# Split weights of k and q stored during the first MLP, and attention outputs summed by an accumulating DMA

## The chip, the cores and the metric

The kernel runs on one core of one Trainium2 chip. The metric is the device time of one execution in microseconds. Engines: PE is the matrix engine (TensorE), DVE the vector engine, ACT the scalar engine, POOL is GpSimd, and SP is the queue that issues most DMAs. Each engine works off its own instructions in order; semaphores tie them together.

## The reference

A decoder of two layers over 1024 tokens of width 1024, float32. Layer 0 mixes by an S5 state-space block, layer 1 by a stick-breaking attention of 16 heads of 64; each mixer is followed by an MLP with squared ReLU of width 4096, and both by a layer norm on a weighted residual.

```python
x = layer_norm(ALPHA * x + mix, ...)           # after s5_mixer or attention
ff = squared_relu_mlp(x, w1, b1, w2, b2)       # square(relu(x @ w1 + b1)) @ w2 + b2
x = layer_norm(ALPHA * x + ff, ...)
...
k, v = split(x @ w_kv)                         # once, after layer 0
q = (x @ w_q)
z = einsum("qd,kd->qk", qb, kb) * scale        # blocks of 128 queries, per head
log_1mb = where(causal, log_sigmoid(-z), 0)
suffix = cumsum(log_1mb, reverse=True) - log_1mb
w = where(causal, exp(log_sigmoid(z) + suffix), 0)
out = einsum("qk,kd->qd", w, vb)               # heads side by side, then out @ w_out
```

## The kernel before

PE multiplies rounded float32 (fp32r). To keep precision every operand is split into a high part, its cast to fp32r, and a low part, the remainder: `split` (L121) casts on ACT (L122) and subtracts on DVE (L123). Each product is three multiplies: high x high, high x low, low x high. A split weight is one tile of 128 x 2 x 512, both parts side by side, 512 KB; the raw weight is 256 KB.

The stages follow each other: the S5 layer (to about 505 us), the up-projection of the first MLP, `mlp_up` (505 to 807), its down-projection, `Down` (807 to 1117), the projection of v, `VProject` (to 1213), the first projections of k and q (to 1242), the attention loop (to 1668), the out-projection `proj_ln` (to 1762) and the second MLP (to 2419).

**First MLP.** `mlp_up` runs 104 steps; each multiplies x by one operand made from the weights (a plan of seven products for four blocks). Operands are split ahead into slots, eight tiles named "w", four in pool `wa` and four in `wb`, handed out in turn by `sl.next()`. `down.ahead` (L1034) is called at each step and does, beside it, what the down-projection needs: it loads the residual `xm_d` in 16 halves, scales them, adds a bias and stores them back (tiles `d0ya` in the pool `pf`, tag "p", four buffers), and at the end loads the first weights of the down-projection into the same buffers.

**k and q.** `project_all` is a generator of units; `load_p` (L1379) loads a weight of k or q for a pair of heads p raw, in two halves `r_k` or `r_q`, and splits it into two slots of `wa`, one projection ahead of its use. The first, `wk0`, is loaded in `VProject.run` behind the fifth of the last eight multiplies by `w_v`. There are 8 pairs, so 16 weights and 32 splits. 33 units run ahead of the loop, the others inside it.

**Attention loop.** 128 `Step`s, 16 heads x 8 query tiles, a software pipeline. `scores` multiplies q by k (`pz`, L1436 and L1437), ACT makes two sigmoids of it, `qq` (L1438) and `be`, and POOL masks their diagonal blocks (`affine_select`, L1441). `weights`, one step later, runs DVE's product scan over `qq` (L1447) and multiplies `be` by it (L1448). `trans` transposes `be` on PE in pieces (`pt`, L1460) and splits them (`wTh` by ACT, `wTl` by DVE). `out`, once for two query tiles, multiplies by v (`po`, L1474). The high and the low part of v lie side by side as 128 columns, so `po` has two halves of 64 rows: high v times both parts of the weights, and low v times their high part. Their sum is the head's output. ACT copies both to `ob` (L1476), and SP stores them apart to `o_d[0]` and `o_d[1]` in memory (L1478). POOL also issues the loads of v (L1426) and the copies that stack k and q for a head (L1410), into its queue in order.

**Out-projection.** `load_o` (L1499) loads both halves of 128 rows of the output (`ol`), adds them on DVE (L1503) and splits the sum into `oT`. Seven are called during the last part of the loop by `out_ahead`, the others behind it.

What order the instructions have on an engine is set by a scheduler that lays out the program by readiness and by the place in which the code stands.

## Time and profile before

| | us |
|---|---|
| median of 3 runs | 2428.63 |
| lowest, highest | 2428.26, 2428.94 |
| the profiled execution's own time | 2421.34 |
| its span | 2419.6 |
| PE, DVE, ACT, POOL busy in the span | 2274.4, 1842.8, 1211.6, 540.0 |
| mean granted clock of PE | 0.984 |

The profiled execution is one run, 7.3 us under the median of the others; its span is the time from its first instruction to its last. Busy time is time in which an engine had an instruction running; PE is busy for 94% of the span, DVE for 76%, but these are means over stages that are bound in different ways. A row `X <- Y` under waits says that X stood idle and that Y's end let it go.

### The profile page before, as it was taken

To read this page: it belongs to the slowest core of one execution; us is meant where nothing else is said; L and a number is where in the kernel's file an instruction comes from. 1 tells how busy PE (TensorE), PEld (TensorE's weight loads), DVE (VectorE), ACT (ScalarE), POOL (GpSimd) and SP (SyncE) were. 2 spreads that over 40 slices of the span, in tenths; PEclk is the share of its full clock that TensorE was granted. 3 is DMA by queue.
4 is the path that set the end of the run, shared out by engine and by line. 5 is a ranking of instruction groups with operands and counts; after the bars stand their busy time and mean duration, and the time that the engine had idled before them with its cause. 6 is when DMAs were issued, how large, how long until landed. Compare 5 with 4: busy or idle time off the path is not lost.

```text
span 2419.6 us, 32714 instructions
## 1 busy us (share of the span) xinstructions
PE 2274.4 (94%) x11040; PEld 1860.3 (77%) x11040; DVE 1842.8 (76%) x2868; ACT 1211.6 (50%) x2283; POOL 540.0 (22%) x796
## 2 busy tenths in 40 slices
PE   9887799999999999999999999988989999999996
PEld 7666677777888788887888788766767888788885
DVE  8778664797665788789259999897788666687888
ACT  5344452366555444445147667673357555444443
POOL 6556430012112100001134443341002211100001
PEclk9989899999999999999999999999999999999998
DMA  4222131366444755435665555555358444665433
GB/s 148 56 64 58 40 121 62 110 224 232 144 144 165 251 180 166 147 101 147 131 157 118 121 130 125 120 134 187 113 182 290 156 156 146 224 206 165 132 115 106
DMA packets 195161, 349.39 MB, mean 144 GB/s; under 512 B 23216, under 2 KB 66224, under 8 KB 194992
## 3 DMA queue, kind: packets, MB, share of 16 engines
q1 hardware_dynamic: 136112, 246.61, 32.4%
q0 software_dynamic: 58880, 100.69, 15.0%
q8 instruction: 87, 1.43, 0.2%
q14 instruction: 82, 0.67, 0.1%
HBM read 212.96 MB, written 100.66 MB: 130 GB/s over the span
## 4 chain that ended last, share of the span: by engine, by line
PE 64%; DVE 12%; issue 5%; DMA 4%; POOL 2%; ACT 2%; SPq 0%; POOLq 0%; DVEq 0%; ACTq 0%
PE d0M L1096 4%; PE d0M L1097 4%; PE d0M L1098 4%; PE d1M L1096 4%; PE d1M L1098 4%; PE d1M L1097 4%; DVE qq L1447 2%; PE m1A L832 2%; PE m1A L834 2%; PE m1A L833 2%; PE m0A L832 2%; PE m0A L833 2%; PE m0A L834 2%; DVE be L1448 2%; PE po L1474 1%
## 5 line engine op out<-in xcount | busy, mean ns | idle before, releaser
L1447 DVE TENSOR_TENSOR_SCAN qq<-qq 128x128 f32<-128x128 f32 (+7 forms) x128 | 174.2, 1363 | 11.4 <-POOL qq L1441 11.1
L1096 PE MATMUL d1M<-w_d12M,w_d1HM 128*128 128x512 f32 x448 | 174.9, 391 | 3.9 <-DVE d1y L1105 3.9
L1096 PE MATMUL d0M<-w_d02M,w_d0HM 128*128 128x512 f32 x448 | 174.6, 390 | 1.6 <-ACT w_d02M L122 1.2
L1098 PE MATMUL d1M<-w_d12M,w_d1HM 128*128 128x512 f32 x448 | 175.2, 391 | 0.0
L1097 PE MATMUL d1M<-w_d12M,w_d1HM 128*128 128x512 f32 x448 | 174.7, 390 | 0.0
L1097 PE MATMUL d0M<-w_d02M,w_d0HM 128*128 128x512 f32 x448 | 174.5, 389 | 0.0
L1098 PE MATMUL d0M<-w_d02M,w_d0HM 128*128 128x512 f32 x448 | 174.3, 389 | 0.0
L192 POOL TENSOR_TENSOR rsd<-ved,nhalf 128x1 f32<-128x1 f32 x16 | 16.2, 1014 | 621.5 <-DVE ved L190 613.3
L122 ACT CAST w_d1HM<-d1hM 128x512 fp32r<-128x512 f32 x110 | 68.3, 621 | 170.1 <-PE d1M L1098 148.3
L122 ACT CAST w_d0HM<-d0hM 128x512 fp32r<-128x512 f32 x110 | 68.3, 621 | 169.1 <-PE d0M L1098 143.6
L122 ACT CAST wTh<-pt 128x512 fp32r<-128x512 f32 (+1 forms) x192 | 88.0, 485 | 81.4 <-PE pt L1460 80.9
L1460 PE MATMUL pt<-ident,be 128*128 128x128 f32 x576 | 90.5, 281 | 34.8 <-DVE wTl L123 25.8
L1460 PEld LDWEIGHTS pt<-ident,be 128*128 128x128 f32 x576 | 69.7, 143 | 60.9 <-issue 18.5
L123 DVE TENSOR_TENSOR w_d1HM<-d1hM,w_d1HM 128x512 fp32r<-128x512 f32 x110 | 75.9, 690 | 52.4 <-ACT w_d1HM L122 52.2
L123 DVE TENSOR_TENSOR w_d0HM<-d0hM,w_d0HM 128x512 fp32r<-128x512 f32 x110 | 75.9, 690 | 51.6 <-ACT w_d0HM L122 51.5
L123 DVE TENSOR_TENSOR wTl<-pt,wTh 128x512 fp32r<-128x512 f32 (+1 forms) x192 | 99.5, 545 | 9.9 <-ACT wTh L122 9.9
L1448 DVE TENSOR_TENSOR be<-be,qq 128x127 f32<-128x127 f32 (+7 forms) x128 | 99.4, 777 | 7.2 <-POOL be L1441 0.7
L1096 PEld LDWEIGHTS d1M<-w_d12M,w_d1HM 128*128 128x128 f32 x448 | 84.1, 188 | 24.1 <-ACT w_d12M L122 4.3
L1438 ACT ACTIVATE qq<-pz 128x512 f32<-128x512 f32 (+1 forms) x192 | 96.8, 504 | 10.8 <-DVE be L1448 5.6
L1096 PEld LDWEIGHTS d0M<-w_d02M,w_d0HM 128*128 128x128 f32 x448 | 84.1, 188 | 21.4 <-DVE d0y L1105 2.5
L1098 PEld LDWEIGHTS d1M<-w_d12M,w_d1HM 128*128 128x128 f32 x448 | 84.1, 188 | 18.4
L1097 PEld LDWEIGHTS d1M<-w_d12M,w_d1HM 128*128 128x128 f32 x448 | 84.1, 188 | 17.8
(477 smaller groups left out, 7162.4 us busy)
## 6 DMA issues: line engine op xcount, KB each, us to landing
d0hM<-h_d SPq DMA_DIRECT2D x110, 256.0 KB, 2.7
d1hM<-h_d SPq DMA_DIRECT2D x110, 256.0 KB, 2.7
x1ring<-in_w SPq DMA_DIRECT2D x70, 256.0 KB, 3.2
x3ring<-in_w SPq DMA_DIRECT2D x70, 256.0 KB, 3.2
h_d<-m0hs POOLq DMA_DIRECT2D x64, 256.0 KB, 3.1
h_d<-m1hs POOLq DMA_DIRECT2D x64, 256.0 KB, 2.6
d0r<-in_w SPq DMA_DIRECT2D x58, 256.0 KB, 3.5
d1r<-in_w SPq DMA_DIRECT2D x58, 256.0 KB, 3.7
```

The source lines that it names most:

```text
L122: act.copy(hi, src)
L123: dve.tensor_sub(lo, src, hi)
L832: pe.matmul(ps_, wh, xh[:, k], start=first and k == 0, stop=False, skip_group_check=True)
L833: pe.matmul(ps_, wh, xl[:, k], start=False, stop=False, skip_group_check=True)
L834: pe.matmul(ps_, wl, xh[:, k], start=False, stop=k == 3, skip_group_check=True)
L1096: pe.matmul(ps_, hh[:, tok(t)], wh, start=first, stop=False, skip_group_check=True)
L1097: pe.matmul(ps_, hh[:, tok(t)], wl, start=False, stop=False, skip_group_check=True)
L1098: pe.matmul(ps_, hl[:, tok(t)], wh, start=False, stop=last, skip_group_check=True)
L1438: act.activation(qq[:, s0:s1], pz, AF.Sigmoid, scale=-0.125)
L1447: dve.tensor_tensor_scan(out=rev, data0=rev, data1=rev, initial=1.0, op0=ALU.mult, op1=ALU.bypass)
L1448: dve.tensor_mul(be[:, 0:ns - 1], be[:, 0:ns - 1], qq[:, 1:ns])
L1460: pe.transpose(pt[:, b_], self.be[:, tok(s0 + b_)], ident)
```

## The change

Two parts.

The weights of k and q are split during the first MLP. A job `SplitKQ` is called from `down.ahead`; for each of 32 halves it loads the raw half into a buffer of `pf`, splits it two steps later into a slot of `sl`, and SP stores the 512 KB to `kq_d` in memory. The first load is at step 13, and one follows each two or three steps; the last half is split at step 92. `load_kq` then loads the split weights straight into the slots where `load_p` split them.

The halves of a head's output are added in memory. `o_d` has one half; SP stores the first 64 rows of `ob`, and POOL issues a DMA that adds the other 64 rows to the same place, one `out` later. `load_o` loads once and does not add.

```diff
--- before.py
+++ after.py
@@ -78,7 +78,8 @@
-    o_d = drp.tile([2, D, S], F32, name="o_d")
+    o_d = drp.tile([D, S], F32, name="o_d")
+    kq_d = drp.tile([2, KD, 2, P, 2, HF], F32, name="kq_d")
@@ -995,7 +996,7 @@
-            down.ahead(i, NSTEPS, xo.ring)
+            down.ahead(i, NSTEPS, xo.ring, sl)
@@ -1016,7 +1017,8 @@
-        def __init__(self, l, nm, xd, wb, last, then=None):
+        def __init__(self, l, nm, xd, wb, last, then=None, job=None):
+            self.job = job
@@ -1031,8 +1033,10 @@
-        def ahead(self, i, n, ring):
-
+        def ahead(self, i, n, ring, sl):
+            if self.job:
+                self.job.step(i, self.pf, sl)
@@ -1243,6 +1247,33 @@
+    class SplitKQ:
+        PARTS = [(y, p, c) for p in range(KD) for y in range(2) for c in range(2)]
+        def __init__(self):
+            self.raw = {}
+        def step(self, i, pl, sl):
+            for j, (y, p, c) in enumerate(self.PARTS):
+                i0 = 13 + 5 * j // 2
+                if i == i0:
+                    self.raw[j] = pl.tile([P, HF], F32, tag="p", name=f"kq{j}")
+                    dma.dma_start(self.raw[j], A[("w_k", "w_q")[y]][p][:, half(c)])
+                elif i == i0 + 2:
+                    t = sl.next().tile([P, 2, HF], F32R, tag="w", name=f"w_kq{j}")
+                    split(t[:, 0], t[:, 1], self.raw.pop(j))
+                    dma.dma_start(kq_d[y, p, c], t.bitcast(F32))
+    def load_kq(nm, p):
+        out = []
+        for c in range(2):
+            t = wa.tile([P, 2, HF], F32R, tag="w", name=f"w_{nm}{p}{c}")
+            dma.dma_start(t.bitcast(F32), kq_d["kq".index(nm), p, c])
+            out.append((t[:, 0], t[:, 1]))
+        return by_k(out)
@@ -1291,7 +1322,7 @@
                 if t == 4:
-                    self.wk0 = by_k(load_w(wa, A["w_k"][0], "k0"))
+                    self.wk0 = load_kq("k", 0)
@@ -1346,7 +1377,7 @@
-            down = Down(0, "d0", x_d[0], wb, False, vpr)
+            down = Down(0, "d0", x_d[0], wb, False, vpr, SplitKQ())
@@ -1376,9 +1407,6 @@
-        def load_p(nm, p):
-            return by_k(load_w(wa, A[f"w_{nm}"][p], f"{nm}{p}"))
-
@@ -1387,7 +1415,7 @@
                 if i + 1 < len(seq):
-                    nxt = load_p(*seq[i + 1])
+                    nxt = load_kq(*seq[i + 1])
@@ -1474,11 +1502,16 @@
                 act.copy(ob, fl(po))
-                for b_ in range(2):
-                    dma.dma_start(o_d[b_, self.h * HD:(self.h + 1) * HD, tp_ * 2 * P:(tp_ + 1) * 2 * P],
-                                  ob[b_ * 64:b_ * 64 + 64])
-
-        prs, heads = {p: {} for p in range(KD)}, {}
+                dst = o_d[self.h * HD:(self.h + 1) * HD, tp_ * 2 * P:(tp_ + 1) * 2 * P]
+                dma.dma_start(dst, ob[0:64])
+                osum.append((dst, ob[64:128]))
+        def add_out():
+            dst, src = osum.pop(0)
+            pool.dma_start(dst, src, accum_op=ALU.add)
+        prs, heads, osum = {p: {} for p in range(KD)}, {}, []
@@ -1497,10 +1530,8 @@
         def load_o(k, h):
-            z, z2 = [raws[-1].tile([P, HF], F32, tag="raw", name=f"ol{k}{h}{b_}") for b_ in range(2)]
-            for b_, z_ in enumerate((z, z2)):
-                dma.dma_start(z_, o_d[b_, tok(k), half(h)])
-            dve.tensor_add(z, z, z2)
+            z = raws[-1].tile([P, HF], F32, tag="raw", name=f"ol{k}{h}")
+            dma.dma_start(z, o_d[tok(k), half(h)])
             split(oT[0][:, k, half(h)], oT[1][:, k, half(h)], z)
@@ -1537,7 +1568,10 @@
             if n >= 1 and (n - 1) % 2 == 1:
+                if osum:
+                    add_out()
                 ST[n - 1].out()
+        add_out()
```

On DVE, where one head ends and the next begins in the middle of the attention loop (`qq` and `be` are a step's scan and product, `wTl` the low part of a transposed weight tile, `kl` that of a projected k), before:

```order
L1447 SCALAR_TENSOR_TENSOR qq_0_11694<-qq_0_11694 128x128
L123 TENSOR_TENSOR w_k_11844<-r_k_11845,w_k_11844 128x512
L1448 TENSOR_TENSOR be_0_11693<-be_0_11693,qq_0_11694 128x127
L123 TENSOR_TENSOR wTl_6_11725<-pt_60_11726,wTh_6_11724 128x4x128
L123 TENSOR_TENSOR wTl_6_11725<-pt_64_11733,wTh_6_11724 128x3x128
L123 TENSOR_TENSOR kl_11537<-pjk_11538,kh_11536 128x512
L1447 SCALAR_TENSOR_TENSOR qq_1_11757<-qq_1_11757 128x256
L1448 TENSOR_TENSOR be_1_11756<-be_1_11756,qq_1_11757 128x255
```

and in the changed kernel:

```order
L1475 SCALAR_TENSOR_TENSOR qq_0_11838<-qq_0_11838 128x128
L1476 TENSOR_TENSOR be_0_11837<-be_0_11837,qq_0_11838 128x127
L124 TENSOR_TENSOR wTl_6_11869<-pt_60_11870,wTh_6_11868 128x4x128
L124 TENSOR_TENSOR wTl_6_11869<-pt_64_11877,wTh_6_11868 128x3x128
L124 TENSOR_TENSOR kl_11681<-pjk_11682,kh_11680 128x512
L124 TENSOR_TENSOR wTl_6_11869<-pt_70_11916,wTh_6_11868 128x4x128
L124 TENSOR_TENSOR wTl_6_11869<-pt_74_11923,wTh_6_11868 128x4x128
L1475 SCALAR_TENSOR_TENSOR qq_1_11901<-qq_1_11901 128x256
```

Between the scan and the product of the head's first step the subtraction of `w_k` is gone, and the `wTl` of the head before it now stand ahead of the second scan.

On POOL, in the middle of a head (`qq` and `be` are the masks of steps, `qs` a stacking copy; the brackets list the semaphores that an instruction waits for), before:

```order
L1410 DMA qs_11500<-ql_11173 64x1024 [waits DMASW2_49,DVE_49]
L1441 AFFINE_SELECT qq_4_11509<-qq_4_11509 128x128 [waits Activation_49,Pool_49]
L1441 AFFINE_SELECT be_4_11508<-be_4_11508 128x128 [waits PE_49,Activation_49]
L1441 AFFINE_SELECT qq_5_11563<-qq_5_11563 128x128 [waits Activation_49,Pool_49]
L1441 AFFINE_SELECT be_5_11562<-be_5_11562 128x128 [waits PE_49,Activation_49]
L1441 AFFINE_SELECT qq_6_11597<-qq_6_11597 128x128 [waits DVE_49,Activation_49]
L1441 AFFINE_SELECT be_6_11596<-be_6_11596 128x128 [waits PE_49,Activation_49]
```

and in the changed kernel:

```order
L1438 DMA qs_11650<-ql_11323 64x1024 [waits DMASW5_49,DVE_49]
L1469 AFFINE_SELECT qq_4_11659<-qq_4_11659 128x128 [waits Activation_49,Pool_49]
L1469 AFFINE_SELECT be_4_11658<-be_4_11658 128x128 [waits PE_49,Activation_49]
L1512 DMA o_d<-ob_7_11626 64x256 [waits DMAHW0_49,DMASW6_49]
L1469 AFFINE_SELECT qq_5_11707<-qq_5_11707 128x128 [waits Activation_49,Pool_49]
L1469 AFFINE_SELECT be_5_11706<-be_5_11706 128x128 [waits PE_49,Activation_49]
L1512 DMA o_d<-ob_1_11703 64x256 [waits DMAHW1_49,DMASW7_49]
L1469 AFFINE_SELECT qq_6_11741<-qq_6_11741 128x128 [waits DVE_49,Activation_49]
```

An add of the half before stands between the masks of two steps, behind a wait for its store (`DMAHW`) and for an earlier DMA of POOL's (`DMASW`).

On SP, where the projection of v ends and the first k and q weights are loaded (`x_d` is the stored result of the MLP), before:

```order
L206 DMA x_d<-d0y_6796 128x512 [waits DVE_49]
L133 DMA r_k_10076<-in_w_k 128x512 [waits DMAHW3_49,DVE_49,Activation_49]
L206 DMA x_d<-d0y_6796 128x512 [waits DMAHW2_49,DVE_49]
L133 DMA r_k_10081<-in_w_k 128x512 [waits DMAHW5_49,DVE_49,Activation_49]
L133 DMA r_q_10207<-in_w_q 128x512 [waits DMAHW4_49,DMAHW7_49,DVE_49,Activation_49]
L133 DMA r_q_10212<-in_w_q 128x512 [waits DMAHW1_49,DVE_49]
```

and in the changed kernel, where `r_ao` are the first weights of the out-projection:

```order
L207 DMA x_d<-d0y_6989 128x512 [waits DMAHW2_49,DVE_49]
L134 DMA r_ao_15219<-in_sb_out 128x512 [waits DMAHW5_49,DVE_49,Activation_49]
L1273 DMA w_k_10268<-kq_d 128x1024 [waits DMAHW4_49,PE_49]
L1273 DMA w_k_10270<-kq_d 128x1024 [waits PE_49]
L1273 DMA w_q_10393<-kq_d 128x1024 [waits DMAHW6_49,PE_49]
L1273 DMA w_q_10395<-kq_d 128x1024 [waits DMAHW7_49,PE_49]
```

The raw loads waited for their own buffers, which DVE and ACT free; the loads of split weights wait for PE, the last user of the slot.

## Rows read from the trace of the kernel before

**Rows 1.** The sums by stretch of time of the whole core: stretch, its length in us, then busy us and number of instructions of PE, PEld, DVE, ACT and POOL, then the granted clock, the DMA engines' busy share and GB/s. Six stretches: the start of the first MLP, its steady part, the first projections, four head pairs of the attention loop, its tail, and the start of the out-projection.

```profile
505.00:580.00 75.00, 70.15 (x300) 54.21 (x299) 61.95 (x101) 51.78 (x93) 15.29 (x28) 1.00 0.84 289
580.00:800.00 220.00, 220.00 (x944) 176.72 (x943) 131.95 (x197) 122.84 (x202) 41.55 (x77) 1.00 0.43 148
1213.00:1242.00 29.00, 29.00 (x126) 23.09 (x125) 6.64 (x10) 6.20 (x11) 8.33 (x14) 1.00 0.96 217
1300.20:1508.20 208.00, 197.87 (x1186) 168.43 (x1186) 195.72 (x257) 146.42 (x354) 86.90 (x185) 1.00 0.55 122
1590.00:1668.00 78.00, 59.62 (x350) 47.49 (x349) 74.31 (x98) 52.38 (x127) 32.15 (x53) 0.93 0.50 129
1668.00:1715.00 47.00, 44.17 (x184) 33.22 (x183) 23.74 (x36) 10.11 (x17) 0.00 (x0) 1.00 0.65 221
```

**Rows 2.** The groups of instructions of DVE from 1300.2 to 1508.2 us, four head pairs: line, operation and tile, count | busy us, mean ns | idle us before it and what ended it.

```profile
L1447 DVE TENSOR_TENSOR_SCAN qq<-qq 128x512 f32<-128x512 f32 (+3 forms) x64 | 87.2, 1363 | 3.0 <-POOL qq L1441 2.6
L123 DVE TENSOR_TENSOR wTl<-pt,wTh 128x256 fp32r<-128x256 f32 (+3 forms) x96 | 49.7, 545 | 4.2 <-ACT wTh L122 4.2
L123 DVE TENSOR_TENSOR w_k<-r_k,w_k 128x512 fp32r<-128x512 f32 x8 | 5.4, 675 | 0.0
L123 DVE TENSOR_TENSOR w_q<-r_q,w_q 128x512 fp32r<-128x512 f32 x8 | 5.4, 673 | 0.0
```

**Rows 3.** What PE waited for in the same four pairs: line <- what ended the wait: us in total, times, longest.

```profile
PE pt L1460 <- DVE wTl L123: 9.4, 12, 1.8
```

**Rows 4.** The timeline of DVE near 1491 us: start, us, instruction.

```profile
1490.48 1.07 DVE L1448 TENSOR_TENSOR be<-be,qq 128x767 f32<-128x767 f32 x1
1491.48 0.68 DVE L123 TENSOR_TENSOR wTl<-pt,wTh 128x512 fp32r<-128x512 f32 x1
```

**Rows 5.** The timeline of PE at the same place; in brackets the idle time before and what ended it.

```profile
1492.30 0.30 PE L1460 MATMUL pt<-ident,be 128*128 128x128 f32 x1 [1.65 <-DVE wTl L123]
```

**Rows 6.** The views of the tiles w_k and w_q from 1242 to 1600 us, their DVE rows: count, ns shortest/median/longest, first and last start.

```profile
L123 DVE TENSOR_TENSOR w_k<-r_k,w_k x12: 664/668/685, 1253.9 to 1508.3; 128x512 fp32r<-128x512 f32 x12
L123 DVE TENSOR_TENSOR w_q<-r_q,w_q x12: 660/682/687, 1266.7 to 1534.1; 128x512 fp32r<-128x512 f32 x12
```

**Rows 7.** What PE waited for from 1242 to 1590 us, the attention loop without its tail.

```profile
PE pt L1460 <- DVE wTl L123: 17.9, 19, 2.9
```

**Rows 8.** The groups of DVE from 1590 to 1668 us, the tail.

```profile
L1503 DVE TENSOR_TENSOR ol<-ol,ol 128x512 f32<-128x512 f32 x6 | 4.3, 716 | 0.0
```

**Rows 9.** What PE waited for from 1590 to 1668 us.

```profile
PE pt L1460 <- DVE wTl L123: 7.9, 6, 4.2
PE pt L1460 <- DVE be L1448: 6.9, 8, 1.8
```

**Rows 10.** The view of the tile ol over the whole run: the sums of the halves (ns shortest/median/longest, first and last start), and the landing of its loads.

```profile
L1503 DVE TENSOR_TENSOR ol<-ol,ol x16: 661/692/903, 1558.0 to 1700.7; 128x512 f32<-128x512 f32 x16
DMA to landing us min/median/max: 2.5/3.6/6.7
```

**Rows 11.** What PE waited for from 1668 to 1765 us, the out-projection.

```profile
PE aopy L117 <- ACT oT_h L122: 2.3, 2, 1.9
```

**Rows 12.** The view of the tile ob, a head's output on its way to memory: its copy out of PSUM, and the landing of its 128 stores.

```profile
L1476 ACT COPY ob<-po x64: 369/373/466, 1250.0 to 1667.8; 128x256 f32<-128x256 f32 x64
DMA to landing us min/median/max: 1.9/2.4/5.9
```

**Rows 13.** The view of line 1410, DMAs that POOL issues beside the attention loop: issue time in ns of one group.

```profile
L1410 POOL DMA_DIRECT2D khs<-kh x32: 516/520/557, 1225.4 to 1602.2; - x32
```

**Rows 14.** The timelines of ACT, SP, POOL and DVE between 1459.7 and 1468 us, middle of a head.

```profile
1459.75 0.37 ACT L1476 COPY ob<-po 128x256 f32<-128x256 f32 x1
1460.15 1.09 SPq L1478 DMA_DIRECT2D o_d<-ob  x2
1462.27 0.29 POOL L1441 TENSOR_SCALAR_AFFINE_SELECT be<-be 128x128 f32<-128x128 f32 x1
1464.35 0.29 POOL L1441 TENSOR_SCALAR_AFFINE_SELECT qq<-qq 128x128 f32<-128x128 f32 x1 [1.79 <-ACT qq L1438]
1465.97 2.01 DVE L1447 TENSOR_TENSOR_SCAN qq<-qq 128x896 f32<-128x896 f32 x1
```

**Rows 15.** What DVE waited for from 1300.2 to 1508.2 us.

```profile
DVE qq L1447 <- POOL qq L1441: 2.6, 10, 0.4
```

**Rows 16.** The timelines of ACT, DVE and PE where the V projection ends and the first k projection begins.

```profile
1208.41 1.33 ACT L122 CAST w_k<-r_k 128x512 fp32r<-128x512 f32 x2
1209.07 1.40 DVE L123 TENSOR_TENSOR w_k<-r_k,w_k 128x512 fp32r<-128x512 f32 x2
1213.12 0.39 PE L108 MATMUL pjk<-d0xo_h,w_k 128*128 128x512 f32 x1
```

**Rows 17.** The DMA issues from 1205 to 1242 us: tile, queue, count, size, median us to landing.

```profile
v_d<-vt POOLq DMA_DIRECT2D x2, 512.0 KB, 4.6
r_k<-in_w_k SPq DMA_DIRECT2D x4, 256.0 KB, 4.3
```

**Rows 18.** The view of the tile w_m01M, one operand of the first MLP: its casts and one of its multiplies, with first and last start.

```profile
L122 ACT CAST w_m01M<-m0sM x64: 600/623/662, 503.2 to 779.4; 128x512 fp32r<-128x512 f32 x64
L832 PE MATMUL m0C<-x1B,w_m01M x64: 393/396/497, 513.8 to 798.1; 128*128 128x512 f32 x64
```

**Rows 19.** What POOL waited for from 1300.2 to 1508.2 us.

```profile
POOL v L1426 <- PE pz L1437: 14.8, 9, 2.2
```

## The prediction

> **What bounds the kernel now.** I began with the busy times by stage, because the kernel is a chain of stages with different limits. In the steady part of the first MLP PE is busy for all of its 220 us while DVE works for 132 [rows 1]: the stage is TensorE's, and DVE and ACT have room. In four head pairs of the attention loop it is otherwise: DVE 195.7 of 208 us (94%), PE 197.9 (95%). Two engines are nearly full, so the next question is which of them waits for which. What PE waits for there is one thing, 9.4 us in all: the transposes `pt` wait for DVE's `wTl` [rows 3]. One such place shows how. DVE's `wTl` ends at 1492.16, and PE, idle for 1.65 us, starts its next transpose at 1492.30 [rows 4, 5]; DVE had been working off its queue, in which scans, products and splits stand in a row. So DVE bounds the loop, by a little, and PE is the floor right under it. In the tail (1590 to 1668) the projections have run out: DVE is at 74.3 of 78 us, PE at 59.6 [rows 1], and PE's waits are for `wTl` and `be`, 14.8 us [rows 9]. There DVE alone is the bound. From 1668 on PE leads again (44.2 of 47).
>
> **Attention loop: 24 splits leave DVE.** The weights of k and q are split by one cast on ACT and one subtraction on DVE. Twelve of each fall after 1242 us [rows 6]: 12 x 0.668 + 12 x 0.682 = 16.2 us of DVE. In the four pairs they are 5.4 + 5.4 = 10.8 us of 195.7 [rows 2], or 2.7 us a pair of 52 us. The order of the changed kernel has none of them there. If DVE were the only bound, all 16.2 us would come out. But PE can give back at most what it waits for: 17.9 us from 1242 to 1590 [rows 7], 9.4 of 208 in the four pairs. After the change a pair holds 46.2 us of DVE (195.7 - 10.8, over 4) and 49.5 us of PE, so DVE's total falls under PE's, and the waits that stay are those from local bunching: a long scan in front of a `wTl`. I take two thirds of 16.2, 11 us; the bounds are 6 (about a third) and 16 (all of it, and nearly all of PE's waits). A pair should fall from 52 to about 50.2 us.
>
> **Tail: the sums of the halves leave DVE.** Six additions `ol` stand in the tail [rows 8] and one at 1558, 7 x 0.716 = 5.0 us on the bounding engine. I take 4, bounds 2 to 5. The other nine stand after 1662, in the stretch where PE leads; with them go 9 loads of 256 KB. PE waits there 2.3 us for `oT_h` [rows 11], which is cast from a finished sum, and the loads land in 3.6 us at the median and 6.7 at most [rows 10]. A chain shorter by one addition and one of two loads should give about 2.5 us; bounds 0 and 4.
>
> **What is added in the loop: 64 accumulating DMAs on POOL.** The first half of a head's output is still stored by SP, the second is added by a POOL DMA one step of two query tiles later. It must wait for the store's landing, and POOL works in order, so behind a waiting add stand the affine selects of the next query tiles, and behind these DVE's scans. No row shows an accumulating DMA. The nearest is an issue of `khs`, 520 ns each [rows 13], and 64 of these are 33 us on an engine that is busy 87 of 208 us. The wait is bounded by the stores' landing, 1.9 at best, 2.4 median, 5.9 us at most [rows 12]. One add followed through: `ob` is copied by 1460.12, its stores are issued from 1460.15, so the first is down at about 1462.6. In the new order the add stands behind the `be` select that ends at 1462.56; it would issue at 1462.6 and be through by 1463.1, before the next select at 1464.35 is ready. The scan behind that starts at 1465.97 [rows 14]. So it costs nothing, and a landing of 5 us would just reach the scan. Laying the 40 adds of the loop on the old times in this way, I get scans delayed by 1.0 us in all at a landing of 2.4 us, 8.8 at 3.5, 15.0 at 4.2 and 22.8 at 5.0. Over 64 adds that is 1.6, 14, 24 and 36 us. The median decides, since the stores do not change and the traffic of the loop falls by nothing large: 2 us, bounds 1 and 9. Today DVE waits 2.6 us for POOL's selects in four pairs [rows 15], so there is a little slack, not much.
>
> **First k projection: a load of 512 KB where a split was.** Before, ACT casts `w_k` from 1208.41, when its slots come free, DVE subtracts until 1210.47, and PE takes it at 1213.12 without a gap [rows 16]. After, an SP load into the slot starts when the slot comes free and must land. A 512 KB transfer at that time takes 4.6 us (`v_d`), a 256 KB one 4.3 (`r_k`) [rows 17], so 1208.4 + 4.3 to 4.6 is 1212.7 to 1213.0 when it is alone. DMA is 0.96 busy in the next stretch [rows 1], and 1.3 us more is easily lost. I take 0.7 us, bounds 0 and 1.3; the second half is needed 2.8 us later and is covered. The Trainium skill ("DMA: Bandwidth & Descriptors", section "Anatomy of one DMA — SWDGE (gpsimd) path") fits a transfer at 2.0 us plus its bytes over 436e3 a us, an estimate of 3.2 us for 512 KB; by that the weights would be there at 1211.6 and this term would be 0, the forecast 0.7 us lower. The rows of 4.6 us, with other queues at work, speak against it here.
>
> **First MLP: 32 splits and 25 MB move in.** Each costs ACT 0.62 and DVE about 0.69 us, 20 and 22 us over about 223 us in which DVE had 88 and ACT 97 to spare per 220 [rows 1]. The cover is PE's lead in operands: `w_m01M` is first cast at 503.2 and last at 779.4, and its multiplies by `x1B` run from 513.8 to 798.1 [rows 18], 10 to 19 us behind. Loads and stores add 32 x 768 KB = 25 MB, some 110 GB/s over 223 us, to 148 GB/s at a share of 0.43; the sum, about 258, is below the 289 GB/s at 0.84 that the start of the same stage runs at while PE is 70 of 75 us busy [rows 1]. The `xm_d` rows share their four buffers with the raw weights and so spread out of that dense start into the steady part. I cost it at 0, bounds a gain of 2 (from the thinner start) and a loss of 5 (its idle time in 75 us, once more).
>
> **Sum.** 11 + 4 + 2.5 - 2 - 0.7 - 0 = 14.8 us. The profiled execution took 2421.3 us (span 2419.6) and would take 2406.5; it lies 7.3 us under the median of the runs, 2428.6, so the median becomes 2413.8, say **2414**. Its own bounds: 16 + 5 + 4 + 2 - 1 = 26 gives 2403, 6 + 2 + 0 - 9 - 1.3 - 5 = -7 gives 2436, both with every term at its end at once.
>
> **Rivals.** *The adds hold POOL up: slower.* The mechanism is the one above: the add waits for the store in POOL's queue, affine selects stand behind it, DVE starves. For it: POOL already stands still in front of a DMA whose wait is not over (14.8 us before `v` loads [rows 19]), with selects behind. Against: landings of 2.4 us. It decides when the 64 waits cost more than 16.8 + 4.9 us, 0.34 us an add, at a landing near 4 us. At 5 us the loss is 36 us: 2428.6 - 16.8 + 36 = 2448; at 4.2, 2436. The Trainium skill ("DMA: Bandwidth & Descriptors", section "Anatomy of one DMA — SWDGE (gpsimd) path") says that DMA engines never wait on semaphores and that the wait is held on the issuing sequencer before dispatch; the trace agrees, as POOL's 14.8 us in front of `v` show.
>
> *PE is the floor already.* The DVE work goes, but the waits of `pt` are set by the latency of single chains, and only a third of them goes: 6 + 3 + 1 less 0.7 gives about 2419. For it: PE at 95%. Against: DVE's unbroken row in front of the wait [rows 4].
>
> *The relief turns into waits on ACT or POOL.* DVE then idles where it split before, and only the tail gains, 3 us: 2425.6. For it: DVE's waits for `wTh` are already 4.2 us [rows 2]. Against: they are 2% of the stretch.
>
> *The first MLP pays.* PE is full there, so a late operand is a loss one for one; with 256 GB/s of bursts and one of eight slots taken, 8 us lost in 223 gives 2422.
>
> **Chances.** Forecast 0.66; PE's floor 0.10; first MLP 0.07; no relief 0.07; adds slower 0.07; gain above the forecast's range (all of DVE's time comes out) 0.03. A measurement of this kernel tells 0.2%, 4.9 us, from no change: faster is under 2423.8, slower above 2433.5. Faster is 0.66 + 0.10 + 0.05 + 0.03 = 0.84, within it 0.07 + 0.02 + 0.01 = 0.10, slower 0.06. The range takes in the forecast, PE's floor and the MLP's price: 2407 to 2424.
>
> **What would show it.** In the changed kernel's trace: no w_k or w_q subtraction after 1100 us, and pairs of about 50 us between `v` loads; PE's wait for `wTl` well under 9.4 us in four pairs; POOL's adds at about 0.5 us each and DVE's wait for POOL's `qq` still under 5 us in four pairs (20 us would show the slower rival); PE still full in the steady first MLP; the first `pjk` within 1.3 us of the last `pv`; 16 loads of `ol`, not 32. The prediction is wrong if the pairs stay near 52 us with DVE idle, if the store-to-add wait is over 4 us, or if the first MLP is longer by more than 5 us.

## The result, and the profile after

The changed kernel takes 2446.57 us (median of 6 runs, 2443.32 to 2459.23), the kernel before 2428.45 in the runs beside them (6 runs): 1.0089 times as long, 95% interval 1.0075 to 1.0103. That is slower, and outside the range. The profiled execution's span grew from 2419.6 to 2441.6 us. Cut into stages at the first and last multiply of each stage's tiles in the timeline, in us (the first MLP from the last multiply of the S5 layer's out-projection, at 474.4 in the kernel before; the expectations of e1 to e4 count it from its own first multiply, 3.7 us later, as 329 and 346):

| stage | before | after |
|---|---|---|
| first MLP (to the first `d0M`) | 332.8 | 349.8 |
| down-projection | 309.4 | 309.1 |
| v projection (to the first `pjk`) | 96.5 | 94.8 |
| loop (to the last `pjq`) | 376.2 | 381.3 |
| tail of the loop (to the last `po`) | 78.4 | 82.8 |
| out-projection (to the first `m1A`) | 88.2 | 84.9 |

In single profiles the S5 layer and the second MLP, which no edit touches, differ by up to 7 us between kernels, so a stage's difference of 2 or 3 us says nothing alone. Each profile is one execution: that of the kernel before lies 2 to 7 us under the medians of its runs, that of e2 (below) 10 us above its median, those of e7 and e8 7 and 5 us under theirs. Two losses are larger than such differences: 17 us in the first MLP, and 9.5 in loop and tail where a gain of 13 was forecast.

The sums by stretch, of the steady first MLP and of four head pairs, columns as in [rows 1]:

```profile
580.00:820.00 240.00, 227.50 (x954) 180.56 (x953) 153.67 (x238) 142.13 (x244) 41.46 (x77) 0.99 0.72 253
1318.40:1530.00 211.60, 197.02 (x1184) 167.94 (x1184) 186.55 (x240) 137.93 (x336) 116.37 (x215) 1.00 0.64 140
```

PE, full there before, is idle for 12.5 us of the first stretch. Four pairs took 211.6 us against 208, though DVE has 9 us less to do. What PE waited for in the first MLP (505 to 824 us):

```profile
PE m0A L833 <- DVE m0hA L930: 7.9, 4, 2.2
PE m0A L833 <- ACT m0kM L914: 5.1, 3, 2.2
PE m0C L833 <- ACT m0kM L914: 3.6, 2, 1.8
```

16.6 us, against 3.8 for the same in the kernel before, all for `m0kM` and `m0hA`, the evictions of its products from PSUM. These are ACT's and DVE's work. What held ACT there, 580 to 820 us:

```profile
ACT w_m01M L123 <- DMA kq_d<-w_kq: 39.5, 16, 5.4
```

A cast of an MLP operand stood for 39.5 us, 16 times, in front of ACT's queue and waited for the landing of a store of split weights. One of them, in the timelines of SP, ACT and PE:

```profile
659.00 0.33 SPq L1267 DMA_DIRECT2D kq_d<-w_kq  x1
659.03 0.62 ACT L123 CAST w_kq<-kq 128x512 fp32r<-128x512 f32 x1
664.25 0.62 ACT L123 CAST w_m01M<-m0sM 128x512 fp32r<-128x512 f32 x1 [4.59 <-DMA kq_d<-w_kq]
664.77 0.58 ACT L914 COPY m0kM<-m0C 128x512 f32<-128x512 f32 x1
660.44 0.39 PE L835 MATMUL m0C<-x1T,w_m01M 128*128 128x512 f32 x1
665.40 0.50 PE L833 MATMUL m0C<-x1B,w_m01M 128*128 128x512 f32 x1 [1.78 <-ACT m0kM L914]
```

and the store in the chain of waits:

```profile
659.00 5.17 DMA kq_d<-w_kq
```

The store leaves at 659.00 and lands at 664.17. Until then ACT does nothing, since the cast at 664.25 needs the slot that the store still reads. The copy of a finished product, `m0kM`, could run from 660.83, when the last multiply of `m0C` ends, and stands one place behind the cast; PE gets its bank back 1.78 us too late. Between 580 and 820 us there are seven such waits of PE, 12.4 us. The first multiply after each lasts 0.50 us or more in place of 0.40 [rows 18]. After two of them, of 2.19 and 2.10 us, seven more lasted 0.63 us each, at a granted clock of 0.55, near the lower of its two levels (1.2 of 2.4 GHz); after another of 2.19 us, at 695.84, the clock stayed. The stretch behind the first:

```profile
605.80:609.20 3.40, 3.38 (x9) 2.63 (x10) 3.37 (x7) 2.67 (x5) 0.00 (x0) 0.55 0.45 134
```

By the starts of the multiplies the slower ones cost about 4 us (an estimate), so waits and slow multiplies together make up the stage's 17 us.

In the loop, what PE and then DVE waited for in the four pairs (before: [rows 3, 15]):

```profile
PE pt L1488 <- DVE wTl L124: 12.8, 13, 1.7
PE pt L1488 <- POOL be L1469: 1.2, 1, 1.2
```

```profile
DVE qq L1475 <- POOL qq L1469: 8.1, 14, 1.5
```

PE's wait for `wTl` is not smaller but larger, 12.8 us against 9.4, and DVE's wait for the masks went from 2.6 to 8.1. The view of the tile `ob` has the adds and the landings (before: [rows 12]), and POOL's waits (1242 to 1700 us) have its idle time in front of the adds:

```profile
L1512 POOL DMA_DIRECT2D o_d<-ob x64: 813/863/1098, 1269.9 to 1698.8; - x64
DMA to landing us min/median/max: 1.9/2.7/8.3
```

```profile
POOL o_d L1512 <- DMA o_d<-ob: 66.2, 27, 9.4
```

and the timelines of SP, POOL and DVE show one add in the middle of the loop:

```profile
1365.83 0.45 SPq L1506 DMA_DIRECT2D o_d<-ob  x1
1366.45 0.29 POOL L1469 TENSOR_SCALAR_AFFINE_SELECT be<-be 128x128 f32<-128x128 f32 x1
1370.37 0.86 POOL L1512 DMA_DIRECT2D o_d<-ob  x1 [3.62 <-DMA o_d<-ob]
1370.96 0.59 POOL L1469 TENSOR_SCALAR_AFFINE_SELECT qq<-qq 128x128 f32<-128x128 f32 x1
1371.59 1.02 DVE L1475 TENSOR_TENSOR_SCAN qq<-qq 128x384 f32<-128x384 f32 x1 [1.53 <-POOL qq L1469]
```

SP stores the first half at 1365.83, POOL's add behind it waits for the landing until 1370.37 (the view gives 3.62 us of idle time before it), and takes 0.86 us to issue. The masks of two steps come after it, and DVE's scan starts after 1.53 us of waiting for `qq`.

At the first k projection nothing was lost:

```profile
1223.27 1.03 SPq L1273 DMA_DIRECT2D w_k<-kq_d  x2
1227.74 0.40 PE L120 MATMUL pv<-w_v,d0xo_l 128*128 128x512 f32 x1
1227.97 0.40 PE L109 MATMUL pjk<-d0xo_h,w_k 128*128 128x512 f32 x1
```

The loads leave at 1223.27, the last `pv` is followed by the first `pjk` at the usual distance of 0.23 us. In the out-projection PE's wait for `oT_h` is gone [rows 11]; what is left of the waits for `aopy`:

```profile
PE aopy L118 <- DVE y L758: 0.9, 2, 0.6
```

### The profile page after: what moved, and what is told of

The parts are those of the page before. It is cut to its first block, busy times and chain, and to the rows that moved or that the text cites. A ratio compares the mean times of both kernels' runs of the same rounds, so it can differ in the third digit from the quotient of the medians.

```text
span 2441.6 us, 32823 instructions
## 1 busy us (share of the span) xinstructions
PE 2280.4 (93%) x11040; PEld 1868.2 (77%) x11040; DVE 1833.2 (75%) x2852; ACT 1207.2 (49%) x2283; POOL 595.0 (24%) x860
## 3 DMA queue, kind: packets, MB, share of 16 engines
q0 software_dynamic: 64000, 104.88, 16.6%
## 4 chain that ended last, share of the span: by engine, by line
PE 57%; DVE 12%; DMA 8%; issue 7%; POOL 3%; ACT 3%; SPq 0%; POOLq 0%; DVEq 0%; ACTq 0%
PE d0M L1100 4%; PE d0M L1102 4%; PE d0M L1101 4%; PE d1M L1100 4%; PE d1M L1102 4%; PE d1M L1101 4%; PE m1A L833 2%; DMA kq_d<-w_kq 2%; PE m1A L835 2%; PE m1A L834 2%; PE po L1502 2%; DMA o_d<-ob 2%; DVE qq L1475 2%; PE pt L1488 1%; DVE be L1476 1%
## 5 line engine op out<-in xcount | busy, mean ns | idle before, releaser
L123 ACT CAST wTh<-pt 128x512 fp32r<-128x512 f32 (+1 forms) x192 | 87.5, 484 | 92.9 <-PE pt L1488 92.3
L1476 DVE TENSOR_TENSOR be<-be,qq 128x127 f32<-128x127 f32 (+7 forms) x128 | 99.2, 776 | 11.6 <-POOL be L1469 3.9
```

The costliest lines, as they stand in the source:

```text
L123: act.copy(hi, src)
L1476: dve.tensor_mul(be[:, 0:ns - 1], be[:, 0:ns - 1], qq[:, 1:ns])
```

## The experiments

Median and ratio to the kernel before, with its 95% interval, then stages from one profile in us (first MLP / loop / tail / out-projection; before 332.8 / 376.2 / 78.4 / 88.2). The diffs further down are excerpts; a line in them without a sign says which run it is.

| run | us | ratio | stages |
|---|---|---|---|
| e1_split_only | 2449.06 | 1.0104 (1.0085 to 1.0122) | 353.0 / 382.7 / 78.9 / 88.0 |
| e2_add_only | 2435.98 | 1.0057 (1.0039 to 1.0074) | 336.7 / 391.3 / 81.9 / 85.0 |
| e3_own_tile | 2457.54 | 1.0139 (1.0114 to 1.0164) | 357.0 / 381.5 / 79.9 / 85.9 |
| e4_own_tile_no_add | 2458.84 | 1.0143 (1.0122 to 1.0164) | 359.6 / 383.7 / 78.6 / 87.9 |
| e5_split_no_store | 2422.11 | 0.9986 (0.9977 to 0.9996) | 328.8 / 378.1 / 77.9 / 87.3 |
| e6_traffic_only | 2444.78 | 1.0080 (1.0065 to 1.0095) | 351.8 / 376.8 / 78.0 / 87.1 |
| e7_pool_store | 2436.86 | 1.0046 (1.0030 to 1.0061) | 334.3 / 386.3 / 78.3 / 87.2 |
| e8_late_add | 2434.16 | 1.0040 (1.0024 to 1.0056) | 335.1 / 385.2 / 79.5 / 86.1 |
| e9_pool_traffic | 2452.70 | 1.0107 (1.0083 to 1.0131) | 361.9 / 377.8 / 77.9 / 86.1 |
| e10_pool_job | 2478.12 | 1.0214 (1.0182 to 1.0246) | 376.5 / 385.5 / 77.9 / 86.4 |
| e11_double_split | 2426.47 | 1.0005 (0.9991 to 1.0019) | 333.1 / 378.9 / 78.6 / 87.6 |
| e12_residual_tile | 2426.26 | 1.0003 (0.9990 to 1.0016) | 339.1 / 376.6 / 79.4 / 86.8 |
| e13_paced_no_res | 2436.91 | 1.0042 (1.0027 to 1.0057) | 345.2 / 376.1 / 78.2 / 87.6 |
| e14_no_res | 2417.72 | 0.9958 (0.9945 to 0.9971) | 326.8 / 375.9 / 78.6 / 87.3 |
| e15_paced | 2450.53 | 1.0095 (1.0080 to 1.0111) | 358.7 / 376.3 / 78.3 / 87.5 |
| e16_adds32 | 2412.72 | 0.9947 (0.9930 to 0.9964) | 331.9 / 372.5 / 76.1 / 83.4 |
| e17_copies_no_res | 2417.00 | 0.9964 (0.9952 to 0.9975) | 328.1 / 376.7 / 79.4 / 86.6 |
| e18_three_pt | 2421.30 | 0.9978 (0.9967 to 0.9989) | 333.8 / 371.6 / 79.5 / 86.9 |

### The two parts apart

```diff
 e1: the changed kernel with
+                for b_ in range(2): dma.dma_start(o_d[b_, ...], ob[b_ * 64:b_ * 64 + 64])
+            dve.tensor_add(z, z, z2)
 e2: the changed kernel with
+            nxt = load_p(*seq[i + 1])        # raw load and split, no SplitKQ
```

> The changed kernel with both halves of a head's output stored by SP and added on DVE as before; the weights of k and q still split in the first MLP. In the changed kernel the first MLP was 16.8 us longer and the attention stage 9.4 us. Theory (two separate losses: casts in the first MLP held by the landing of the stores, and POOL's adds in the loop): the first MLP stays about 17 us longer, the attention stage gets shorter than before by about 11 us, in all about 2433 us. Rival (the adds cost little, and taking the splits out of the loop gains little): the attention stage stays near its 464 us, in all about 2444 us.

> The kernel before with the accumulating DMA alone; weights of k and q split in front of each projection as before. Theory: the first MLP takes its old 329 us; the adds hold up the masks on POOL and cost the loop some 20 us with DVE's splits still in it, of which the sums that leave the tail and the out-projection give back 3 to 7: 2440 to 2447 us. Rival (adds cheap): 2422 to 2428 us.

The first MLP lost 20 us in e1, where 17 were expected. The loop did not gain the 11 us: it took 382.7, and loop and tail together 461.6, as the rival had it (near 464; before 454.6). Without splits and without adds it is no shorter than before. And e1, which leaves the adds out, is no faster than the changed kernel (1.0104 against 1.0089, intervals overlapping): its loss is the first part's. Four pairs of e1, and what PE waited for in them:

```profile
1322.68:1533.17 210.49, 197.21 (x1185) 168.49 (x1185) 186.65 (x241) 138.11 (x337) 87.29 (x185) 1.00 0.57 141
```

```profile
PE pt L1488 <- DVE wTl L124: 10.4, 12, 1.8
PE pt L1488 <- POOL be L1469: 2.4, 4, 0.6
```

DVE works 9 us less than before and is idle for 11.6 us more, in a stretch 2.5 us longer; its waits for `wTh` grew from 4.2 [rows 2] to 9.8. PE's waits for `wTl` are what they were. Over the whole loop (1232.8 to 1615.7 us) PE's waits account for the 6.5 us that it took more; in the kernel before they were 17.9, 0.3 and none:

```profile
PE pt L1488 <- DVE wTl L124: 20.1, 19, 2.9
PE pt L1488 <- POOL be L1469: 3.3, 6, 0.6
PE pz L1464 <- DMA qs<-qh: 1.6, 1, 1.6
```

e2 fell between its two expectations. The adds alone cost the kernel 12.8 us by the medians. In e2's profile the loop is 15 us longer, but that execution lay 10 us above the median; in the profile of e8, which differs little (see below), it is 9 us longer.

### Does DVE bound the loop?

```diff
                 split(t[:, 0], t[:, 1], r)
+                dve.tensor_sub(t[:, 1], r, t[:, 0])     # the same again; kernel before
```

> The kernel before, but the subtraction that makes the low part of a k or q weight is done twice; 30 more instructions of 0.68 us on DVE, 24 of them in the loop, 16 us in all. Theory (these instructions stand in gaps of DVE, and the loop's time is set by the chain through masks, scan, product, transposes and their low parts): 0 to 5 us more, 2425 to 2430. Rival (DVE at 94% is the bound, as predicted): 11 to 16 us more, 2436 or later.

No difference that the interval shows, 1.0005 (at most 4.6 us), as the theory said. In four pairs of e11 DVE was 202.56 of 208.00 us busy, 97%. In its profile PE's waits for `wTl` in the loop were 23.2 us against 17.9 and the loop 2.7 us longer, so the added work may not be free; but 16 us of it cost a small part of that at most, and 24 fewer in e1 gained nothing. DVE was 94% busy and still not the bound. Of the 19 waits in [rows 7], 18 end at a `wTl` directly behind a scan and a product, and in none is a split of `w_k` or `w_q` among the four instructions in front of that `wTl`. At the place of [rows 4] the scan in front of the product is

```profile
1488.62 1.75 DVE L1447 TENSOR_TENSOR_SCAN qq<-qq 128x768 f32<-128x768 f32 x1
```

What PE waits for is one chain:

```diff
-        pss = mkpool(ph, "pss", 3, PSUM)
-        pst = mkpool(ph, "pst", 2, PSUM)
+        pss = mkpool(ph, "pss", 2, PSUM)
+        pst = mkpool(ph, "pst", 3, PSUM)
```

> The kernel before, with three PSUM tiles for the transposes of the loop in place of two, and two for the scores in place of three. PE's 17.9 us of waits in the loop are transposes that wait for the low part of two pieces before, which stands behind a scan and a product in DVE's queue. Theory (that chain, not DVE's total, sets the loop): PE's waits for it fall by half or more, the loop gets 5 to 10 us shorter if two tiles are enough for the scores, 2417 to 2423. Rival (scores are held up instead): as before or slower.

```profile
PE po L1474 <- DVE wTl L123: 12.1, 14, 3.3
PE pt L1460 <- DVE wTl L123: 1.2, 1, 1.2
```

With a third tile for the transposes, PE's 17.9 us of `pt` behind `wTl` [rows 7] became 1.2; 12.1 us came back in front of `po`, which needs the same `wTl`. The loop took 4.6 us less and the kernel 0.22% less, 2421.30 us, within what the theory gave. So a part of the wait was for a tile, which is freed by a `wTl` that stands behind a scan and a product; the larger part came back at the next user of the same `wTl`.

### The first MLP: slots, work, traffic or a held queue?

```diff
 e3, e4 (e4 with SP's stores and DVE's sums of e1): the job without slots
+                    split(hi, r.bitcast(F32R), r)       # hi: a tile of its own; low part over the raw
+                    dma.dma_start(kq_d[y, p, c, :, 0], hi.bitcast(F32))
+                    dma.dma_start(kq_d[y, p, c, :, 1], r)
 e5: before, with the job that does not store
-                    dma.dma_start(kq_d[y, p, c], t.bitcast(F32))
 e6: before, with the job that does not split
+                    for b_ in range(2): dma.dma_start(kq_d[y, p, c, :, b_], r)
```

> The changed kernel, but the split weights don't take one of the eight slots of the first MLP: the high part goes to a tile of its own, the low part over the raw weight, and both are stored apart as 256 KB. The traffic is the same, and no operand waits for a slot that a store still reads. Theory (a cast of an operand is queued on ACT behind the landing of a store that holds its slot): the first MLP falls back to about 329 us, PE's 16.6 us of waits there to about 4, in all about 2430 us. Rival (the added traffic of 25 MB delays loads and evictions by itself): the first MLP stays near 346 us, in all about 2446 us.

> The same with the halves stored by SP and added on DVE as before, so neither loss is left. Theory: first MLP 329 us, attention stage about 11 us shorter than before, in all about 2416 us. Rival (traffic): about 2433 us. Rival (splits out of the loop gain little): about 2426 us.

> The kernel before, with the job in the first MLP that loads the 32 raw halves and splits them into slots, but stores nothing; the loop loads and splits its weights as before, so what the job makes is thrown away. First MLP before: 332.8 us; with split and store 350 to 360. Theory A (ACT's queue is held by the landing of the stores): without stores the first MLP takes 333 to 336 us, in all about 2428. Theory B (the 40 us of ACT and DVE work and the slots themselves cost the time): 345 us or more, in all about 2440.

> The kernel before, with the job's DMAs alone in the first MLP: the 32 raw halves are loaded and each is stored twice as 256 KB, straight from the buffer it was loaded into; nothing is split there, and the loop works as before. The bytes are those of the changed kernel. Theory A (ACT held by a wait for a landing): little is lost, since no operand's cast waits for these stores; the first MLP takes 333 to 338 us, some of it from the residual's tiles, which share the four buffers. Theory C (the traffic itself delays the loads and stores that the stage lives on): 345 us or more, in all about 2440.

e5 clears the work and the slots, as theory A said: with all 32 splits the stage was even 4 us shorter. The stores cost the time. But e3 and e4, without slots, missed both of their expectations and were worse, and e6, without splits, lost 19 us, the figure of theory C, which looked like the traffic itself. In all three, ACT still stood at a landing. In e3 its casts waited 25.6 us for the store of the one tile; in e6 it was the scaling of the residual, whose buffers the job shares:

```profile
613.07 0.63 ACT L1047 ACTIVATE d0ya<-d0ya 128x512 f32<-128x512 f32 x1 [7.07 <-DMA d0ya<-xm_d]
613.60 0.57 ACT L914 COPY m0kM<-m0C 128x512 f32<-128x512 f32 x1
```

7.07 us in front of `d0ya`, with the copy of a product right behind. So none of these runs had taken the mechanism away. Not every landing at the head of ACT's queue is paid for, though. In e5 it waited for loads of the residual too, but for 3.2 us at most, and PE's waits for evictions were 1.0 us in all:

```profile
ACT d0ya L1047 <- DMA d0ya<-xm_d: 16.1, 11, 3.2
```

In the changed kernel the longest such wait was 5.4 us. How long one may be before PE pays for it, no run shows. Two more runs moved the DMAs to POOL, and a third gave the residual its own tile without a job:

```diff
 e9: e6 with pool.dma_start throughout, residual in a tile of its own (ypf, one buffer)
 e10: the same, splits by POOL, weights loaded split in the loop
+                    pool.tensor_copy(hi, r); pool.tensor_sub(r.bitcast(F32R), r, hi)
 e12: before, with ypf alone
-                    self.yt = self.tile(self.pf, f"ya{q}", "p")
+                    self.yt = self.tile(self.ypf, f"ya{q}", "p")
```

> As the run with the job's DMAs alone, but all of them are issued by POOL, and the residual's halves have a tile of their own, so that no instruction of ACT, DVE or SP waits for a store of the job. The bytes are the same. Theory A (an engine's queue is held by the landing of a store): the first MLP is at most 336 us, in all about 2425. Theory C (the traffic itself): 345 us or more, in all about 2440, as in the run that issued them from SP (351.8 us).

> The whole first part of the change, with the halves of the outputs stored and added as before, but the job's loads, casts, subtractions and stores are all POOL's, and the residual has its own tile. Theory A: the first MLP is at most 336 us; the loop has no splits, and by the earlier run without them (382.7 us against 376.2) it gains nothing, so in all 2425 to 2432. Rival (loop gains once the first MLP is undisturbed): 2415 or less. Theory C: 2440 or more.

> The kernel before, with one tile of its own for the 16 residual halves that the first MLP scales and stores back, in place of four shared buffers. It spreads them over the MLP; before, all 16 ran between 515 and 570 us. In the run that split without storing, where they were spread too, the first MLP took 328.8 us against 332.8. Theory (the bunch at the start costs these 4 us): first MLP 329 us, in all 2420. Rival (the 4 us were chance): no difference.

e9 (361.9 us) and e10 (376.5) came out in theory C's range, but decide nothing: the residual's own tile, meant to free ACT, held it for 50.0 us in e9, 45.3 in e10 and 26.1 in e12. In e12 the kernel was unchanged, as the rival said, so the 4 us of e5 were not reproduced; the first MLP of its profile, 6 us longer, is from an execution 3 us above the median. So the residual's steps were left out:

```diff
 e13 to e17 (not e16); e15 keeps the residual, e14 has no job
-            if 0 <= q < 16:
+            if 0 <= q < 16 and self.l:
 e13, e15: e6 by POOL, from one buffer of the job's own
 e17: nothing but copies, three for each part
+                    dma.dma_start(dst, h_d[max(0, i // 7 - 2), (3 * j + b_) % 7])
```

> The kernel before, with the job's DMAs alone (32 raw halves loaded, each stored twice), from one buffer of its own and all issued by POOL, so that they come one at a time. Left out: the scaling and biasing of the 16 residual halves in the first MLP, loads and stores included, so that no instruction of ACT or DVE there waits for a DMA of the added traffic. The run with the same left out and no job is its control. Theory A (queues held at a landing): the first MLP within 3 us of the control's. Theory C (the traffic as such): 10 us or more above the control.

> Control: the kernel before without the scaling and biasing of the 16 residual halves in the first MLP (left out, with their loads and stores). First MLP 326 to 330 us, since the bunch at its start goes.

> The job's DMAs alone, one at a time on POOL from a buffer of their own, with the residual halves as in the kernel before. Theory A: the residual's halves run in the first 70 us and their casts on ACT wait for loads that share the DMA engines with the job; some 3 to 8 us are lost there and nothing after 600 us, first MLP 336 to 341. Theory C: 345 or more.

> As the control without the residual's halves (left out, with their loads and stores; first MLP 326.8 us), with 96 copies of 256 KB from memory to memory added in the first MLP, the number of 256 KB pieces that the changed kernel moves there. They copy h_d rows that were stored some steps before, touch no tile of an engine, and no ACT, DVE or POOL instruction waits for them. Theory A (queues held at a landing): first MLP within 3 us of the control. Theory C (the traffic as such lengthens the landings of the loads and stores that the stage lives on): 10 us or more above it.

The control e14 took 326.8 us, as expected. e13 lost 18 us against it, and e15, with the residual, 26 against the kernel before: theory C's figures again. This time POOL's queue was held by the job (153.2 us of waits for its landings in e13), the stores `h_d` stood behind it, and DVE's evictions waited for tiles that these had not yet emptied; DVE's row for it in the first MLP, in e13 and in e15:

```profile
DVE m0hA L930 <- DMA h_d<-m0hA: 34.2, 10, 6.0
DVE m0hA L930 <- DMA h_d<-m0hA: 38.4, 10, 6.9
```

In e17 nearly nothing of an engine waits for the copies (ACT 1.4 us). The sums by stretch for 60 us of e17 and of its control e14, those of the stage in e17 and in the changed kernel, and e17's DMA issues in the stage:

```profile
580.00:640.00 60.00, 60.00 (x259) 48.20 (x258) 36.96 (x55) 33.58 (x55) 11.38 (x21) 1.00 0.79 271
```

```profile
580.00:640.00 60.00, 60.00 (x259) 48.22 (x258) 37.42 (x56) 33.05 (x55) 11.33 (x21) 1.00 0.42 145
```

```profile
505.00:820.00 315.00, 313.38 (x1346) 250.85 (x1344) 201.08 (x305) 179.61 (x299) 60.89 (x112) 1.00 0.73 251
505.00:820.00 315.00, 297.57 (x1256) 235.65 (x1255) 211.66 (x331) 191.22 (x332) 56.76 (x105) 0.99 0.72 252
```

```profile
kq_d<-h_d SPq DMA_DIRECT2D x64, 256.0 KB, 4.8
h_d<-m0hs POOLq DMA_DIRECT2D x64, 256.0 KB, 4.6
x1ring<-in_w SPq DMA_DIRECT2D x61, 256.0 KB, 4.1
```

The DMA engines were 0.79 busy at 271 GB/s against 0.42 at 145, the stage's own transfers landed in 4.1 and 4.6 us (2.9 and 2.7 in the control; 3.7 and 4.1 in the changed kernel), and PE stayed full: 328.1 us against 326.8. Over the stage e17 moves as much as the changed kernel, 251 GB/s against 252. So this traffic by itself costs about 1 us, and theory C falls. What costs is an instruction that waits long for a landing at the head of an in-order queue in front of evictions. This is put together from e5 (work and slots without stores), e17 (traffic without waits, and without the residual) and the rows; no run has the job with its stores and with every queue free.

### The adds: wait or issue?

```diff
 e7: before, second half
+            pool.dma_start(o_d[1, ...], src)          # no accum_op; sums by DVE
 e8: e2 with four buffers for ob
-                if osum:
+                if len(osum) >= 3:
 e16: e2 with one tile ob for two output steps
+                if tp_ % 2:
+                    dma.dma_start(dst, ob[0:64]); osum.append((dst, ob[64:128]))
```

> The kernel before, with the second half of a head's output stored by a plain POOL DMA into its own place, at the spot in the program where the accumulating DMA stood; the sums are again DVE's. POOL has the same 64 issues but need not wait for the landing of the first half. With the accumulating DMA alone the kernel took 2436 us, 13 more than before, and the loop up to the last q projection 391 us against 376. Theory (the wait for the landing in front of the masks costs the loop): 2424 to 2429 us, loop near 378. Rival (the issues themselves, 0.86 us each, cost it): 2435 us or more, loop near 390.

> The accumulating DMA alone again, but issued three output steps after its half was stored, with four buffers for it instead of two, so that the store has long landed. Theory (the wait costs the loop): the loop takes about 378 us and the kernel 2420 to 2425, under the time before, since the sums leave the tail and the out-projection. Rival (the issues cost it): 2434 us or more.

> The accumulating DMA alone, but one for two output steps: 32 stores and 32 adds of 128 KB in place of 64 of 64 KB. With 64 adds the loop took 391.3 us to the last q projection, with 64 plain POOL stores 386.3, before 376.2. Theory (each DMA instruction on POOL costs the loop about the same, by its issue of 0.86 us and its wait): half of the 15 us, loop near 384, in all about 2429. Rival (the cost hangs on the bytes or on the landing alone): loop near 391.

e7 and e8 came out as their rivals said, near 2435 us; e16 was faster than both of its expectations. The plain store takes 0.54 us to issue, the add 0.86, and the plain one waits for `ob` instead of a landing; first e7's rows, then POOL's waits before the adds in e2, e8 and e16:

```profile
L1515 POOL DMA_DIRECT2D o_d<-ob x64: 527/543/559, 1249.6 to 1677.0; - x64
```

```profile
POOL o_d L1515 <- ACT ob L1507: 81.0, 36, 8.1
```

```profile
POOL o_d L1515 <- DMA o_d<-ob: 73.3, 31, 9.4
```

```profile
POOL o_d L1515 <- DMA o_d<-ob: 63.1, 32, 9.0
```

```profile
POOL o_d L1518 <- DMA o_d<-ob: 24.9, 11, 13.5
```

e7 did not isolate the issue, since the store was placed where it waits for ACT (81.0 us in all). e8 did not remove the wait: it was 63.1 us, and an add still started 3.7 us behind its store at the median, as in e2, so the scheduler had moved it forward again, however late it stands in the code. With half the instructions the waits fell from 73.3 us in 31 places to 24.9 in 11, the loop from 391.3 to 372.5, and the kernel to 2412.72 us. The bytes are the same, so they are not what costs. Which of the rest it is stays open: issues and waits fell together, SP's stores are halved too, and `ob` has room for four steps as in e8, where that alone gained nothing clear. Nor is it explained that the loop is 3.7 us under that of the kernel before. e16 beats both kernels: 0.53% under the one before.

## Why the prediction was wrong, step by step

Three terms of the sum failed: 11 us for the loop, 0 for the first MLP and 2 for the adds. The first MLP is the dearest, 17 us; the loop is the one whose reasoning was wrong at the start.

**Attention loop, 24 splits: the step that failed first.** "So DVE bounds the loop, by a little" was read from 94% busy time. The rows that it stood beside showed a product in front of the late `wTl`, and in front of that stood a scan, not a split. Leaving the splits out gave nothing (e1), doubling the subtractions nothing that the medians show (e11). Four pairs took 52.9 us each with DVE idle, which the prediction itself had named as a sign of being wrong. The third rival, that the relief turns into waits and idle time of DVE, was right here, and it had 0.07. That the loop was even 6 to 9 us longer without splits (e1, e4, e10) was seen three times. In e1 PE's waits account for it, most of it for `wTl` and the masks; why these come later is not explained: the order of the engines' work changes and the loads double, and no run parts the two.

**First MLP, costed at 0.** The engines had the time and the DMA engines the bandwidth, as the prediction said: e5 and e17 show both. What it left out is the order of ACT's queue. It counted PE's lead over its operands as cover; but the casts that wait stand in front of evictions, which have no such lead. ACT waited 39.5 us for landings there, PE 16.6 us for evictions. The rival "the first MLP pays" named the right place with 8 us and expected late operands; it is 17, by late evictions.

**Adds on POOL, costed at 2 us.** The mechanism was the rival's, and the size was off on both sides of the sum: the issue is 0.86 us and not 0.52, and "the median decides" did not hold. SP's stores landed in 2.1 us at the median in the changed kernel, under the 2.4 that were priced, but 16 of the 64 took more than 3.5 us (counted from the issues in the trace), a landing that the prediction itself prices at 14 us, and POOL stood 66.2 us in front of its adds. Alone the adds cost the kernel 12.8 us (e2). Together with the first part they cost nothing more in the loop, 381.3 against 382.7, and 4 in the tail. The Trainium skill ("DMA: Bandwidth & Descriptors", section "Anatomy of one DMA — SWDGE (gpsimd) path") says that a DMA's wait on a semaphore is held on the issuing sequencer before dispatch. The rows agree: the add at 1370.37 held POOL for 3.62 us, and the masks came behind it.

**Tail and out-projection.** 6.5 us were forecast from the sums that leave DVE. In e16, where the adds hold POOL little, it is 2.3 + 4.8 = 7.1. In the changed kernel the tail lost 4.4 instead, and the out-projection gained 3.3 where 2.5 were forecast.

**First k projection.** 0.7 us forecast, none lost. The weights had 4.7 us between issue and use, and such loads landed in 4.5 us at the median (1220 to 1260 us), which sufficed.

## What to carry to other kernels

A busy share near 100% does not make an engine the bound: look at what stands directly in front of the late instruction, and only that is worth moving. Work for an idle engine is not free when it brings a wait for a DMA's landing into a queue that also evicts results: give such an instruction a tile that has long been free, or a queue with nothing urgent behind it (no run here did this for the first MLP, so what it would gain is not shown). For DMAs issued by a compute engine's queue, count instructions and waits, not bytes: half as many adds, with the same bytes, turned a loss of 13 us into a gain of 14, the sums that leave DVE included.

## What the runs showed of the hardware

An accumulating DMA of 64 x 256 float32 took POOL 0.86 us to issue, a plain one of the same shape 0.54. Adding 96 transfers of 256 KB to a stage raised the landing of the stage's stores from 2.7 to 4.6 us, and cost about 1 us where no compute engine's queue stood behind them.
